# Two Strassen pairs in place of four plain blocks in a decoder layer's output projection

## The chip, the cores and the metric

One core of one Trainium2 chip runs the whole kernel. The metric is the device time of one execution in microseconds (us); the time of the kernel before is the median of three runs. The engines are written as in the profile: PE (TensorE's matmuls), PEld (its weight loads), DVE (VectorE), ACT (ScalarE), POOL (GpSimd) and SP (which issues the weight transfers). Each runs its own list of instructions strictly in order and waits on the others through semaphores.

## The reference, cut to what matters

A decoder layer for 256 tokens, width 2048: a SwiGLU feed-forward, a mixer of attention and a gated recurrence, a second SwiGLU feed-forward, a gated embedding. The part that changes is the end of the mixer and the way into the second feed-forward:

```python
merged = sigmoid(gate_a) * (out_a @ w_up_a) + sigmoid(gate_b) * (out_b @ w_up_b)   # 256 x 2048
x = x + merged @ w_out                                                            # 2048 x 2048
h = rmsnorm(x, ffn2_norm)                                                         # mean over 2048
x = x + 0.5 * (silu(h @ w_gate) * (h @ w_up)) @ w_down                            # 5632 wide
```

## The kernel before, in words

Tokens are two tiles of 128 (t = 0, 1); the 2048 columns of x are four blocks of 512 (nb = 0 to 3), each of them two SBUF tiles x[0][nb] and x[1][nb]. All weights are f32 and arrive on SP's queue as tiles `raw` of 128x1024: 256 rows of the weight by 512 columns. To keep f32 accuracy each operand is split in two fp32r parts: ACT casts a weight to `whi` (line 127), DVE subtracts to get `wlo` (line 128), and the product is act_hi·whi + act_lo·whi + act_hi·wlo. Rings of buffers limit how far this runs ahead: 8 raw tiles, 5 whi and 5 wlo. So the cast of weight i+5 has to wait until PE has read whi of a weight that is done with. `Weights.next` prepares up to 4 weights ahead (AHEAD), and one call of it also runs the tasks that `W.later(n, ...)` has put n weights into the future.

There are two ways to multiply.

- `block_a` makes one block of 512 columns in two PSUM banks of the ring `acc` (4 banks), with 12 matmuls of 128x512 for each weight tile.
- `strassen_group` makes two blocks at once (gate and up of a feed-forward, or two neighbouring blocks). The contraction is cut in four quarters by PATTERN "PSPS". A P quarter is plain: 4 weight tiles, 12 matmuls each. An S quarter is Winograd's form of Strassen's method on 2 x 2 x 2 sub-blocks: seven products ("roles") instead of eight, each with 6 matmuls, so 42 instead of 48; four of the weights in it are sums, which DVE forms in place (line 111), and the seven split weights again need whi and wlo. Its activations (`A.roles`) include four sums too, in hi and lo (tiles `as`). The group has eight accumulators: P1, P2, Q3, Q6 in the ring `acc` and Q7, Q5, P4, PE in the ring `misc` (4 banks too, shared with all transposes). At its end ACT copies P1 and DVE combines the banks (lines 422 and 432) into the result.

The norm before the second feed-forward is hidden as follows. `scaled_stage` takes the sum of squares of each finished x block on ACT (`square_sum`, line 275). After three of the four blocks it forms a provisional scale s3 from the three (lines 546 to 549), and `scaled_parts` scales x by it (`xs`, line 371), transposes it on PE (`tx`, line 363), multiplies by the gain and splits into hi and lo (`ap`), for quarters 0, 1 and 2; quarter 3 follows after the fourth block. The exact factor, the full rms over s3, is applied later to the outputs of the feed-forward.

The order of the instructions on each engine comes from the scheduler of the framework, which lists them by priority and by its own estimates and gives out the buffers of a ring in that order; the weight preparation has a raised priority. The order is fixed before the kernel runs.

Of the kernel before, what the change touches and what calls it, by code (L numbers as in the profile page):

```python
# [10 lines left out]
F32 = mybir.dt.float32  # L11
# [4 lines left out]
ALU = mybir.AluOpType  # L16
AX = mybir.AxisListType
# [133 lines left out]
GATES = ((0, 1), (), (2,), (3,))  # L151


def weight_order():
# [49 lines left out]
    for nb in range(4):  # L204
        block("w_out", nb)
# [11 lines left out]
def decoder_layer(ctx: ExitStack, tc: tile.TileContext, io, out):  # L217
# [148 lines left out]
    def scaled_parts(A, q, s, gain, kind):  # L366
# [22 lines left out]
        if kind == "P":  # L389
            return  # L390
        a11, a21, a12, a22 = (quarter[:, k, :, t] for k in range(2) for t in range(2))
        a5, a6, a7, a3 = (full[1][:, i] for i in range(4))
# [3 lines left out]
        nc.scalar.copy(hi, full[1])  # L396
        nc.vector.tensor_tensor(lo, full[1], hi.bitcast(F32), op=ALU.subtract)
        raw = lambda k, t: lambda c: tuple(A.plain[q][k][:, c, h, t * P:(t + 1) * P] for h in range(2))
        mix = lambda i: lambda c: (hi[:, i, c], lo[:, i, c])
        A.roles[q] = (raw(0, 0), raw(1, 0), mix(3), mix(1), mix(2), mix(0), raw(1, 1))  # L400
# [133 lines left out]
    def scaled_stage(stage, gain):  # L534
# [390 lines left out]
    mT = {}  # L925
    sga, sgb = {}, {}
    A2, on_block, left2 = scaled_stage("f2", gains["ffn2"])
    for nb in range(4):
# [174 lines left out]
```

## Time and profile before

| | |
|---|---|
| median of 3 runs | 2187.78 us (2187.15 to 2188.99) |
| the profiled execution | 2186.81 us, of which the span 2184.9 us |
| busy in the span: PE, PEld | 2164.2 us (99%), 1779.4 us (81%) |
| busy in the span: DVE, ACT | 1756.6 us (80%), 1208.0 us (55%) |
| output projection (w_out), PE | 1274.8 to 1366.6 us |
| the second feed-forward's first group on PE | 1366.6 to 1408.5 us |

A busy PE counts overlapped matmuls: one lasts about 0.39 us in the records, and the next one starts about 0.23 us after it. What a stage costs is therefore read from the distance of starts. Rows of the timeline give start, duration, engine, line, operation, names out<-in, shapes, how many were merged, and in brackets the engine's idle time before and what ended it.

### The profile page before, as it was taken

What the parts mean: (1) busy time and instruction counts of PE and PEld (TensorE: products, weight loads), DVE (VectorE), ACT (ScalarE), POOL (GpSimd) and SP (SyncE); (2) the same over time, 40 slices, a digit from 0 to 9 for tenths busy, and PEclk for the clock granted to TensorE, in tenths of its full rate; (3) what the DMA queues carried; (4) which work ended last, traced back from release to release, by engine and by line L of the source; (5) the groups of instructions that cost most, each with busy time, mean ns of one, the idle gap of its engine ahead of it and who ended that gap; (6) DMA issues with size and microseconds to landing.
All of it is one profiled execution on the core that took longest, in us unless ns stands there. A gap on an engine that the chain in (4) does not pass through costs nothing.

```text
span 2184.9 us, 28075 instructions
## 1 busy us (share of the span) xinstructions
PE 2164.2 (99%) x10352; PEld 1779.4 (81%) x10352; DVE 1756.6 (80%) x2066; ACT 1208.0 (55%) x1547; POOL 14.0 (1%) x28
## 2 busy tenths in 40 slices
PE   8999999999999999999999999999999999999998
PEld 7888888888888888887888888878888888888877
DVE  7997979789796998787664556998896979889586
ACT  8554645445456666556444445665554545555664
POOL 0000000000000000000000000000000000000000
PEclk9999999999999999999999999999999999999999
DMA  9464655646466447444565665447555464656552
GB/s 339 164 231 156 233 165 218 220 166 231 157 245 194 161 178 249 146 129 147 155 192 187 190 191 180 167 170 249 185 215 183 176 210 172 246 182 219 175 196 101
DMA packets 117928, 418.96 MB, mean 192 GB/s; under 512 B 13728, under 2 KB 13984, under 8 KB 117792
## 3 DMA queue, kind: packets, MB, share of 16 engines
q1 hardware_dynamic: 116928, 415.83, 56.1%
q8 instruction: 81, 1.33, 0.2%
q10 hardware_dynamic: 864, 1.35, 0.2%
q14 instruction: 55, 0.45, 0.1%
HBM read 415.03 MB, written 2.10 MB: 191 GB/s over the span
## 4 chain that ended last, share of the span: by engine, by line
PE 95%; DVE 2%; DMA 1%; issue 1%; ACT 1%; SPq 0%; POOL 0%; ACTq 0%; POOLq 0%; DVEq 0%
PE ps L419 45%; PE pa L310 14%; PE pa L311 14%; PE pa L316 14%; PE pb L331 3%; PE pb L333 1%; DVE wlo L128 1%; PE tp L353 1%; PE lv L847 1%; PE tx L363 1%; ACT whi L127 0%; DMA raw<-in_ffn_up 0%; PE sc L765 0%; DMA raw<-in_ffn_gate 0%; DMA x<-in_x 0%
## 5 line engine op out<-in xcount | busy, mean ns | idle before, releaser
L127 ACT CAST whi<-raw 128x1024 fp32r<-128x1024 f32 (+1 forms) x931 | 951.1, 1052 | 806.2 <-PE pa L311 385.8
L128 DVE TENSOR_TENSOR wlo<-raw,whi 128x1024 fp32r<-128x1024 f32 (+1 forms) x931 | 1101.5, 1219 | 326.5 <-ACT whi L127 316.7
L419 PE MATMUL ps<-whi,ap 128*128 128x512 f32 x2200 | 573.9, 391 | 2.5 <-DVE ff L422 2.1
L419 PEld LDWEIGHTS ps<-whi,ap 128*128 128x128 f32 x2200 | 410.2, 188 | 91.3 <-DVE ff L422 6.8
L419 PE MATMUL ps<-wlo,ap 128*128 128x512 f32 x1100 | 314.4, 390 | 0.1
L310 PE MATMUL pa<-whi,act 128*128 128x512 f32 x704 | 274.4, 392 | 0.0
L311 PE MATMUL pa<-whi,act 128*128 128x512 f32 x704 | 273.7, 391 | 0.0
L111 DVE TENSOR_TENSOR raw<-raw,raw 128x1024 f32<-128x1024 f32 x200 | 244.6, 1223 | 5.1
L419 PEld LDWEIGHTS ps<-wlo,ap 128*128 128x128 f32 x1100 | 206.3, 188 | 43.3 <-DVE wlo L128 0.5
L419 PE MATMUL ps<-whi,as 128*128 128x512 f32 x800 | 213.8, 391 | 0.9 <-ACT whi L127 0.9
L316 PE MATMUL pa<-wlo,act 128*128 128x512 f32 x704 | 193.9, 391 | 0.0
L419 PEld LDWEIGHTS ps<-whi,as 128*128 128x128 f32 x800 | 149.1, 188 | 35.4 <-ACT whi L127 3.7
L310 PEld LDWEIGHTS pa<-whi,act 128*128 128x128 f32 x704 | 132.0, 188 | 27.5 <-ACT act L355 0.6
L311 PEld LDWEIGHTS pa<-whi,act 128*128 128x128 f32 x704 | 132.1, 188 | 27.1 <-DVE act L356 0.4
L316 PEld LDWEIGHTS pa<-wlo,act 128*128 128x128 f32 x704 | 131.9, 188 | 26.9
L310 PE MATMUL pa<-whi,ap 128*128 128x512 f32 (+1 forms) x384 | 144.7, 381 | 0.0
L311 PE MATMUL pa<-whi,ap 128*128 128x512 f32 (+1 forms) x384 | 141.5, 373 | 0.0
L422 DVE TENSOR_TENSOR ff<-ps,ff 128x512 f32<-128x512 f32 x200 | 128.1, 682 | 0.8
L419 PE MATMUL ps<-wlo,as 128*128 128x512 f32 x400 | 123.5, 390 | 0.0
L316 PE MATMUL pa<-wlo,ap 128*128 128x512 f32 (+1 forms) x384 | 97.6, 372 | 0.0
L419 PEld LDWEIGHTS ps<-wlo,as 128*128 128x128 f32 x400 | 74.9, 188 | 16.0 <-DVE wlo L128 0.6
L310 PEld LDWEIGHTS pa<-whi,ap 128*128 128x128 f32 x384 | 72.4, 189 | 14.1 <-issue 1.1
(250 smaller groups left out, 1740.8 us busy)
## 6 DMA issues: line engine op xcount, KB each, us to landing
raw<-in_ffn_up SPq DMA_DIRECT2D x176, 512.0 KB, 5.2
raw<-in_ffn_down SPq DMA_DIRECT2D x176, 512.0 KB, 5.4
raw<-in_ffn_gate SPq DMA_DIRECT2D x175, 512.0 KB, 4.5
raw<-in_w_ga SPq DMA_DIRECT2D x32, 512.0 KB, 3.5
raw<-in_w_gb SPq DMA_DIRECT2D x32, 512.0 KB, 3.5
raw<-in_w_out SPq DMA_DIRECT2D x32, 512.0 KB, 3.5
raw<-in_ple_gate SPq DMA_DIRECT2D x32, 512.0 KB, 4.6
raw<-in_w_i SPq DMA_DIRECT2D x16, 512.0 KB, 4.2
```

Of the source, the lines that this page charges most:

```text
L111: add = lambda out, a, b: nc.vector.tensor_tensor(out, a, b, op=ALU.add)
L127: nc.scalar.copy(hi[:, c], src[:, c])
L128: nc.vector.tensor_tensor(lo[:, c], src[:, c], hi[:, c].bitcast(F32), op=ALU.subtract)
L310: nc.tensor.matmul(ps[t], ks[:, 0, tok], hi[:, c], start=(j == 0 and c == 0), stop=False)
L311: nc.tensor.matmul(ps[t], ks[:, 1, tok], hi[:, c], start=False, stop=False)
L316: nc.tensor.matmul(ps[t], ks[:, 0, tok], lo[:, c], start=False, stop=(last and c == 1))
L331: nc.tensor.matmul(ps, hi[:, c], mov(c), start=(first and c == 0), stop=False)
L333: nc.tensor.matmul(ps[:, 0:S], lo[:, c], mov(c)[:, 0], start=False, stop=False)
L353: nc.tensor.transpose(pt[:, c, t * P:(t + 1) * P], srcs[t][:, i * P:(i + 1) * P], ident)
L363: nc.tensor.transpose(pt[:, c, t * P:(t + 1) * P], srcs[t][:, i * P:(i + 1) * P], ident)
L419: nc.tensor.matmul(bank(i), stat, mov, start=done[i] == 1, stop=done[i] == todo(i))
L422: nc.vector.tensor_tensor(out, banks[b], other, op=op)
```

## The change

The output projection runs as two `strassen_group` calls: blocks 0 and 1, then blocks 2 and 3. For that `merged` in transposed and split form (tiles mT) is kept as `Operands`, and `role_parts` makes the four activation sums of the S quarters from it (quarter 1 during the up-projections, quarter 3 during the first group). Four weights become seven in each S quarter, so 44 prepared weights take the place of 32. `scaled_stage` gets a parameter: for the second feed-forward the provisional scale now covers the first two blocks (the first group), quarters 0 and 1 are made during the second group, and quarters 2 and 3 after it, during the feed-forward's first group. The two other uses of `scaled_stage` are unchanged.

```diff
+LATE = (3, 3, 3, 2)
...
-    for nb in range(4):
-        block("w_out", nb)
+    for nb in (0, 2):
+        pair(("w_out", nb), ("w_out", nb + 1))
...
+    def role_parts(A, q):
+        full, sums = (atile([P, 4, 2, P], F32, name="af") for _ in range(2))
+        quarter = full.rearrange("p (k c) t n -> p k c t n", k=2)
+        for kp in range(2):
+            v = A.plain[q][kp].bitcast(F32)
+            nc.vector.tensor_tensor(quarter[:, kp].rearrange("p c t n -> p c (t n)"), v[:, :, 0], v[:, :, 1], op=ALU.add)
+        A.roles[q] = sum_parts(A, q, quarter, sums)
...
-            if nb == 2:
-                nc.vector.tensor_reduce(v3, ss[:, :, 0:3], axis=AX.X, op=ALU.add)
-                nc.vector.tensor_scalar(v3, v3, 1.0 / 1536, EPS, op0=ALU.mult, op1=ALU.add)
+            if nb == first - 1:
+                nc.vector.tensor_reduce(v3, ss[:, :, 0:first], axis=AX.X, op=ALU.add)
+                nc.vector.tensor_scalar(v3, v3, 1.0 / (512 * first), EPS, op0=ALU.mult, op1=ALU.add)
...
-                for q in range(3):
+                for q in range(first):
                     W.later(1 + 2 * q, lambda q=q: scaled_parts(A, q, s3, gain, PATTERN[q]))
...
-                W.later(2, lambda: scaled_parts(A, 3, s3, gain, PATTERN[3]))
+                for q in range(first, 4):
+                    W.later(q - 1, lambda q=q: scaled_parts(A, q, s3, gain, PATTERN[q]))
...
-    A2, on_block, left2 = scaled_stage("f2", gains["ffn2"])
+    A2, on_block, left2 = scaled_stage("f2", gains["ffn2"], 2)
...
+        mO.plain[nb] = [atile(name="mT") for _ in range(2)]
         for kp in range(2):
-            mT[2 * nb + kp] = m = atile(name="mT")
-            W.later(3 + kp, lambda m=m, e=e, kp=kp: transpose_split(m, e, kp))
-    for nb in range(4):
-        ps = block_a("w_out", nb, lambda k: mT[k // 2][:, k % 2])
-        for t in range(2):
-            nc.vector.tensor_tensor(x[t][nb], ps[t], x[t][nb], op=ALU.add)
-        on_block(nb)
+            W.later(LATE[nb] + kp, lambda nb=nb, e=e, kp=kp: transpose_split(mO.plain[nb][kp], e, kp))
+        if PATTERN[nb] == "S":
+            W.later(LATE[nb] + 2, lambda nb=nb: role_parts(mO, nb))
+    for nb in (0, 2):
+        def merged(d, t, second, nb=nb):
+            nc.vector.tensor_tensor(x[t][nb + second], d[:, t], x[t][nb + second], op=ALU.add)
+
+        strassen_group(("w_out", nb), ("w_out", nb + 1), mO, PATTERN, merged)
+        on_block(nb)
+        on_block(nb + 1)
```

SP's list of transfers keeps its order to the last row. On PE, DVE and ACT the lists differ only between the end of the up-projections and the first quarters of the second feed-forward. Lines below the new LATE are numbered one higher in the change, those of `strassen_group` 13 higher (L422 is L435, L419 is L432), and L964 is the addition to x. Weights are numbered through: in the change 526 to 547 are the first pair of w_out, 548 to 569 the second, and 570 to 591 the first group of the second feed-forward.

**First place: PE, where the transposes of the scaled x stand.** Before, in w_out's last block (weights 550 to 557, banks pa), after the norm over three blocks:

```order
L316 MATMUL pa_584_11248<-wlo551_11187,mT_527_9661 128x512
L316 MATMUL pa_585_11249<-wlo551_11187,mT_527_9661 128x512
L363 MATMUL tx_590_11262<-ident_64,xs_586_11256 128x128
L363 MATMUL tx_591_11271<-ident_64,xs_586_11256 128x128
L310 MATMUL pa_584_11248<-whi552_11204,mT_536_9832 128x512
L311 MATMUL pa_584_11248<-whi552_11204,mT_536_9832 128x512
```

Two weights of the block, 24 matmuls, stand between the third block's end and the first transpose. In the change, at the start of the second pair (ps_604 and ps_606 are P2 and Q3 in the ring acc, ps_605 and ps_607 are P4 and PE in the ring misc, which the tx tiles share):

```order
L432 MATMUL ps_604_11189<-whi548_11088,mT_526_9660 128x512 x4
L432 MATMUL ps_604_11189<-wlo548_11089,mT_526_9660 128x512 x2
L432 MATMUL ps_604_11189<-whi550_11114,mT_527_9661 128x512 x4
L432 MATMUL ps_604_11189<-wlo550_11115,mT_527_9661 128x512 x2
L432 MATMUL ps_606_11207<-whi549_11101,mT_526_9660 128x512 x4
L432 MATMUL ps_606_11207<-wlo549_11102,mT_526_9660 128x512 x2
L432 MATMUL ps_606_11207<-whi551_11132,mT_527_9661 128x512 x4
L432 MATMUL ps_606_11207<-wlo551_11133,mT_527_9661 128x512 x2
L432 MATMUL ps_618_11296<-whi552_11161,mT_536_9832 128x512 x4
```

```order
L432 MATMUL ps_606_11207<-wlo554_11222,as_544_9936 128x512 x2
L432 MATMUL ps_619_11334<-whi555_11274,as_544_9936 128x512
L364 MATMUL tx_602_11171<-ident_64,xs_598_11165 128x128
L364 MATMUL tx_603_11180<-ident_64,xs_598_11165 128x128
L364 MATMUL tx_602_11171<-ident_64,xs_599_11166 128x128
L364 MATMUL tx_602_11171<-ident_64,xs_598_11165 128x128
```

Each of the first four weights is used for one of its two token tiles only, then 552, 553, 554 and one matmul of 555 follow, then the eight transposes, and only behind them the other halves of 548 to 551 (in ps_605 and ps_607). Until those are done, 548 to 551 hold four of the five whi buffers. The start of the second feed-forward's first group has the same form: 42 matmuls (570 to 573 for one token tile, 574 to 576), then two transposes of x's block 2.

**Second place: DVE around the provisional norm.** Before, after w_out's third block:

```order
L949 TENSOR_TENSOR x12_79<-pa_581_11093,x12_79 128x512
L128 TENSOR_TENSOR wlo555_11295<-raw555_11202,whi555_11294 128x1024
L546 TENSOR_REDUCE v3f2_8541<-ssf2_8539 128x2
L547 TENSOR_SCALAR v3f2_8541<-v3f2_8541 128x2
L549 TENSOR_TENSOR v3f2_8541<-v3f2_8541,s3f2_8540 128x2
L128 TENSOR_TENSOR wlo556_11313<-raw556_11220,whi556_11312 128x1024
```

In the change, after the first pair (L435 forms the last combination, L111 the sums of weights of the next S quarter):

```order
L128 TENSOR_TENSOR wlo553_11204<-raw553_11112,whi553_11203 128x1024
L964 TENSOR_TENSOR x11_78<-ff_575_10787,x11_78 128x512
L435 TENSOR_TENSOR ff_574_10786<-ps_578_10798,ff_574_10786 128x512
L128 TENSOR_TENSOR wlo554_11222<-raw554_11130,whi554_11221 128x1024
L964 TENSOR_TENSOR x10_77<-ff_574_10786,x10_77 128x512
L111 TENSOR_TENSOR raw554_11130<-raw555_11159,raw554_11130 128x1024
L111 TENSOR_TENSOR raw555_11159<-raw552_11099,raw555_11159 128x1024
L559 TENSOR_REDUCE v3f2_8541<-ssf2_8539 128x2
L111 TENSOR_TENSOR raw552_11099<-raw552_11099,raw554_11130 128x1024
L560 TENSOR_SCALAR v3f2_8541<-v3f2_8541 128x2
L111 TENSOR_TENSOR raw553_11112<-raw553_11112,raw552_11099 128x1024
L128 TENSOR_TENSOR wlo555_11275<-raw552_11099,whi555_11274 128x1024
```

The last addition to x (x10) now stands behind wlo554, and the reduction stands ahead of the sum that weight 555 is made of.

**Third place: ACT there.** Before:

```order
L127 CAST whi555_11294<-raw555_11202 128x1024
L275 ACTIVATE junk_583_11242,ssf2_8539<-x12_79 128x512
L371 ACTIVATE xs_586_11256<-x00_73,s3f2_8540 128x512
L127 CAST whi556_11312<-raw556_11220 128x1024
L371 ACTIVATE xs_587_11257<-x10_77,s3f2_8540 128x512
```

In the change:

```order
L127 CAST whi553_11203<-raw553_11112 128x1024
L127 CAST whi554_11221<-raw554_11130 128x1024
L276 ACTIVATE junk_592_11146,ssf2_8539<-x10_77 128x512
L276 ACTIVATE junk_593_11148,ssf2_8539<-x01_74 128x512
L276 ACTIVATE junk_594_11150,ssf2_8539<-x11_78 128x512
L127 CAST whi555_11274<-raw552_11099 128x1024
L372 ACTIVATE xs_598_11165<-x00_73,s3f2_8540 128x512
L372 ACTIVATE xs_599_11166<-x10_77,s3f2_8540 128x512
```

Three sums of squares, the cast of 555 and two scalings of x now stand in a row behind the cast of 554.

More of the change, by code (lines that the diff above doesn't have):

```diff
@@ L390, in scaled_parts, with sum_parts @@
             return
+        A.roles[q] = sum_parts(A, q, quarter, full[1])
+    def role_parts(A, q):
[5 more added lines that the diff above has]
+        A.roles[q] = sum_parts(A, q, quarter, sums)
+    def sum_parts(A, q, quarter, sums):
         a11, a21, a12, a22 = (quarter[:, k, :, t] for k in range(2) for t in range(2))
-        a5, a6, a7, a3 = (full[1][:, i] for i in range(4))
+        a5, a6, a7, a3 = (sums[:, i] for i in range(4))
         for o, u, v in ((a5, a21, a22), (a6, a11, a5), (a7, a21, a11), (a3, a12, a6)):
@@ L395, in scaled_parts @@
         hi, lo = (atile([P, 4, 2, P], name="as") for _ in range(2))
-        nc.scalar.copy(hi, full[1])
-        nc.vector.tensor_tensor(lo, full[1], hi.bitcast(F32), op=ALU.subtract)
+        nc.scalar.copy(hi, sums)
+        nc.vector.tensor_tensor(lo, sums, hi.bitcast(F32), op=ALU.subtract)
         raw = lambda k, t: lambda c: tuple(A.plain[q][k][:, c, h, t * P:(t + 1) * P] for h in range(2))
         mix = lambda i: lambda c: (hi[:, i, c], lo[:, i, c])
-        A.roles[q] = (raw(0, 0), raw(1, 0), mix(3), mix(1), mix(2), mix(0), raw(1, 1))
+        return (raw(0, 0), raw(1, 0), mix(3), mix(1), mix(2), mix(0), raw(1, 1))
     def strassen_group(first, second, A, pattern, post):
@@ L532, in ffn, with scaled_stage @@
                     on_block(nb)
-    def scaled_stage(stage, gain):
+    def scaled_stage(stage, gain, first=3):
         ss = const.tile([P, 2, 4], F32, name=f"ss{stage}")
```

2 lines of the change are left out of this document (1 added, 1 removed).

## The prediction

> **What bounds the kernel now.** I read the page's engine shares, its chain of waits and its costliest groups first, then the busy times of the two stages that change, then the timeline at three places.
>
> ```profile
> PE 2164.2 (99%) x10352; PEld 1779.4 (81%) x10352; DVE 1756.6 (80%) x2066; ACT 1208.0 (55%) x1547; POOL 14.0 (1%) x28
> PE 95%; DVE 2%; DMA 1%; issue 1%; ACT 1%; SPq 0%; POOL 0%; ACTq 0%; POOLq 0%; DVEq 0%
> 1274.60:1366.60 92.00, 91.38 (x418) 75.26 (x417) 53.61 (x62) 49.02 (x68) 0.69 (x1) 1.00 0.59 183
> 1366.60:1408.00 41.40, 41.40 (x187) 34.17 (x187) 37.48 (x40) 27.25 (x36) 0.70 (x1) 1.00 0.42 146
> 1408.00:1450.00 42.00, 41.07 (x183) 33.02 (x182) 41.21 (x43) 24.88 (x28) 0.00 (x0) 1.00 0.53 195
> ```
>
> The last three rows are windows: stretch, its length, busy PE, PEld, DVE, ACT, POOL, then the granted clock. PE sets the end. In w_out (first window) it never stops, and DVE works 53.6 of 92 us; in the groups of the second feed-forward (the other two) DVE works 91 and 98% of the time. So the change moves a stage from the first kind to the second, and both engines must be costed. What a matmul costs:
>
> ```profile
> 1299.38 1.07 PE L316 MATMUL pa<-wlo,mT 128*128 128x512 f32 x4
> 1302.10 1.07 PE L316 MATMUL pa<-wlo,mT 128*128 128x512 f32 x4
> ```
>
> From one weight's wlo part to the next one's is 2.72 us for 12 matmuls: 0.227 us each.
>
> **What it saves.** 32 weights of 12 matmuls are 384; the two groups have 2 x (4 x 12 + 7 x 6) = 180 each, 360. 24 matmuls at 0.227 are **-5.4 us**. Transposes stay 40 in both (8 of merged, 32 of x).
>
> **What it adds to DVE and ACT.** 12 more weights to split, 16 sums of weights, 16 combinations of banks and two sets of activation sums.
>
> ```profile
> L128 DVE TENSOR_TENSOR wlo<-raw,whi 128x1024 fp32r<-128x1024 f32 x65 | 75.0, 1218 | 3.8 <-ACT whi L127 3.6
> L111 DVE TENSOR_TENSOR raw<-raw,raw 128x1024 f32<-128x1024 f32 x24 | 29.3, 1221 | 0.4
> 1405.88 5.76 DVE L128 TENSOR_TENSOR wlo<-raw,whi 128x1024 fp32r<-128x1024 f32 x5
> 1411.56 4.39 DVE L422 TENSOR_TENSOR ff<-ps,ff 128x512 f32<-128x512 f32 x7
> ```
>
> Five splits in 5.76 us start 1.14 us apart; seven combinations in 4.39 us start 0.62 apart; a sum of weights takes 1.22. A steady group of the change, from its first combination to the next group's, has on DVE 22 splits (25.0), 8 sums (9.8), 12 combinations and additions to x (7.4) and the norm and splits of two quarters of x (about 6): 48.2 us, where PE needs 180 x 0.227 = 40.8 plus 16 transposes. So DVE has no slack to repay a late start. For the first group role_parts comes on top (about 4 us) with fewer combinations; the 3.9 us that DVE idled in the second window cover that, and I cost it at 0 (up to 2 if not). ACT gets 12 casts, two copies of a bank and two casts of sums, 16 us, where it worked 49 of 92: nothing away from the joints. The raw transfers stay 32, in the same order.
>
> **What is late: the two joints.** Between two groups the kernel before already waits once:
>
> ```profile
> 1406.89 0.57 ACT L432 COPY ff<-ps 128x512 f32<-128x512 f32 x1
> 1407.37 2.01 ACT L127 CAST whi<-raw 128x1024 fp32r<-128x1024 f32 x2
> 1408.48 1.07 PE L419 MATMUL ps<-whi,ap 128*128 128x512 f32 x4
> 1412.30 1.20 PE L419 MATMUL ps<-whi,ap 128*128 128x512 f32 x4 [0.93 <-DVE ff L422]
> ```
>
> The next group starts at 1408.48. DVE starts the combinations 3.1 us later (1411.56, above), behind the splits of five more weights. PE does 12 matmuls (2.7 us) and needs a bank that the first combination frees: it goes on 3.8 us after the start, 1.1 us late. In the change this joint carries the norm too. Its parts:
>
> ```profile
> 1285.54 0.39 PE L311 MATMUL pa<-whi,mT 128*128 128x512 f32 x1
> 1285.97 1.05 ACT L127 CAST whi<-raw 128x1024 fp32r<-128x1024 f32 x1 [1.27 <-PE pa L311]
> 1287.05 1.23 DVE L128 TENSOR_TENSOR wlo<-raw,whi 128x1024 fp32r<-128x1024 f32 x1 [1.39 <-ACT whi L127]
> 1369.62 0.63 ACT L275 ACTIVATE junk<-x 128x512 f32<-128x512 f32 x1
> 1370.24 1.32 ACT L371 ACTIVATE xs<-x,s3f 128x512 f32<-128x512 f32 x2
> 1370.89 0.15 DVE L280 TENSOR_REDUCE rstdf<-ssf 128x2 f32<-128x8 f32 x1
> 1371.33 0.70 POOL L282 TENSOR_TENSOR rstdf<-rstdf,nhalf 128x2 f32<-128x2 f32 x1 [24.82 <-DVE rstdf L281]
> ```
>
> A cast starts 0.43 us after the start of the last matmul that read its buffer, the split 1.08 after the cast; squares and scalings (junk, xs) take 0.62 each; the reduction 0.15, the power 0.70.
>
> First joint, T = 0 where weight 548 starts, by the lists shown with the change. 548 and 550 run to 2.7, then PE waits to 3.8; 549 and 551 end at 6.5. 548 to 551 keep four whi buffers, so weights now pass one at a time through the fifth: 552's last read of whi starts at 7.2; cast of 553 at 7.65, split at 8.7 (DVE has just done nine combinations and additions, 3.1 + 9 x 0.62 = 8.7); 553's last read at 9.4; cast of 554 at 9.9; DVE does x11 and the last combination to 11.1, the split of 554 to 12.2, x10 to 12.9. ACT squares x10, x01, x11 to 14.9. The reduction goes at 15.0, the sum that 555 needs to 16.3, its cast to 17.4 (the power runs beside it), the two scalings to 18.7, the eight transposes to about 19.4. By then PE has done 43 matmuls and 8 transposes. For a transpose:
>
> ```profile
> L363 PE MATMUL tx<-ident,xs 128*128 128x128 f32 x24 | 3.6, 280 | 0.6 <-ACT xs L371 0.6
> ```
>
> 3.6 us for 24 is 0.15 each, so the work is 9.75 + 1.2 = 10.95 and 8.5 us are lost. Behind it the last four transposes need a misc bank whose DVE reads come behind a split, about 0.5 more: **+9.0 us**.
>
> Second joint, same clock: x12 at 12.9; three squares, the last started at 14.2; first scaling 14.8 to 15.5, second to 16.1 (the factor is known, so no power). The two first transposes start at 15.5 where PE has 42 matmuls (9.5) behind it; with the six others it is at 16.9 for 44 matmuls and 8 transposes, 11.2: 5.7 lost. Then quarter 3's second scaling stands behind two casts and two splits on ACT (0.4), and the cast and split of 580 are late by 0.55 and 0.4: **+7.1 us**. Both sums contain the usual 1.1.
>
> Smaller terms. Before, PE waited 0.6 us for xs (the row above): -0.6. In block 2's up-projections the gate's copy out of its bank (`nat`) now comes four casts later, since it waits for a buffer of the ring of 23 that role_parts fills; so the next product takes the bank that DVE frees behind the last matmul:
>
> ```profile
> 1263.91 0.69 DVE L938 TENSOR_TENSOR mg<-pa,nat 128x512 f32<-128x512 f32 x1 [1.09 <-PE pa L316]
> ```
>
> That read takes 0.69: +0.7, between 0 and 1.
>
> The clock. At the first joint PE idles from 12.9 to 17.5, 4.6 us.
>
> ```profile
> 5.84 0.79 PE L310 MATMUL pa<-whi,hTf 128*128 128x512 f32 x1 [5.84 <-ACT whi L127]
> 6.86 0.63 PE L310 MATMUL pa<-whi,hTf 128*128 128x512 f32 x1
> 7.29 0.63 PE L311 MATMUL pa<-whi,hTf 128*128 128x512 f32 x1
> 9.01 0.40 PE L311 MATMUL pa<-whi,hTf 128*128 128x512 f32 x1
> 2175.25 0.40 PE L316 MATMUL pa<-wlo,ap 128*128 128x256 f32 x2
> 2178.00:2180.00 2.00, 0.00 (x0) 0.00 (x0) 1.30 (x5) 0.83 (x2) 0.55 (x1) 0.95 0.00 0
> 2180.00:2182.00 2.00, 0.00 (x0) 0.00 (x0) 0.05 (x1) 0.50 (x1) 0.00 (x0) 0.50 0.78 294
> ```
>
> After the last matmul (ended 2175.65) the granted clock halves at 2179.8 (0.95 over two us means 1.8 us full), 4.15 us later; matmuls at the very start are 0.43 apart, not 0.227, from 5.84 to about 9.0 us. So the first joint may restart at half rate, 0 to +1.5 us, of which I take **+1.0**; the second idles 2.6 us and should keep its clock, 0. The Trainium skill, "TensorE: Matmul & The Clock Gate", section "What's actually happening", says that the clock falls after at least one idle window of about 3.4 us and that the window runs free. By this the first joint surely pays its 1.5, and the sum would be 0.5 higher; the row here gives a longer delay, so the measured one counts.
>
> **The sum**: -5.4 + 9.0 + 7.1 - 0.6 + 0.7 + 1.0 = **+11.8 us**. Against the profiled execution, 2186.8 (span 2184.9 and 1.9 around it), this is 2198.6; the median of the runs is 1.0 higher, so 2199.6. Bounds of the joints: 1.1 each (the joint before, below), and half-rate restarts in both (2.0 more) with 2 us of late DVE behind each (6 more in all, above). SP's transfers wait for raw buffers that are freed later, not earlier, and land ahead of their use as now.
>
> **The rivals.** *A, forecast: the norm's chain holds PE at both joints*, 2199.6. For it: PE works in order, and the transposes stand ahead of half of four weights. *B, not slower: the scaled x is there when PE gets to the transposes.* The place is the first transpose, the point that decides 9.75 us after the group's end (9.5 at the second); the price is then 1.1 at each joint: -5.4 - 0.6 + 2.2 + 0.7 = -3.1, 2184.7. The kernel before speaks for it, where 24 matmuls nearly covered such a chain; against it, there the chain was without two casts, a split and three additions that wait for a late combination. Its best case, with no wait at all, is 2182.5. *C: DVE's throughput is the bound, not the chain.* Then the second pair and the feed-forward's first group take 48.2 each, the first 41.9 + 0.7; together 139.0, where 91.8 + 41.9 = 133.7 stood: +5.3, 2193.1. For it, the 98% of the last window; against it, DVE itself waits in the chain. *D: the joints are longer*, both restart at half rate and DVE comes later still: +6, about 2206. *E: the compiled work is not what it says*, ruled out by the lists.
>
> **How the numbers follow.** A 0.68, B 0.08, C 0.13, D 0.11. The measurement tells about 0.2% (4.4 us) from no change. Faster needs B's best end: 0.03. Same holds the rest of B and the low end of C: 0.08. Slower: 0.89. The range takes in A and its bounds, most of C and of D: 2191 to 2206; A's own is 2195 to 2203.
>
> **What would show it.** In the profile after: w_out and the first feed-forward group together about 146 us (133.7 before); two PE idle stretches before `tx` of 4 to 5 and 2 to 3 us, released by xs, each with two shorter ones before it, released by whi; the row of tx (L364) with some 7 us of idle, 0.6 before; a granted clock below 1 in the stretch of the first joint; w_out's first pair at about 42 us. If PE passes the transposes without an idle stretch, A is wrong; if DVE is busy all through the joints, it is C.

## The result, and the profile after

The change makes the kernel slower: 2202.78 us in the median of four runs (2201.43 to 2204.20), where the kernel before took 2187.47 beside it. The ratio is 1.0069, with an interval of 1.0057 to 1.0081. That is +15.3 us against a forecast of +11.8; 2202.8 lies in the range (2191 to 2206) and in forecast A's own range (2195 to 2203). Why it is so late is another matter: in the change PE is held as A said, but when e1 below takes that hold away, another wait takes its place and most of the loss stays.

The profiled execution of the change took 2204.06 us with a span of 2202.1. Its first row of engine shares:

```profile
PE 2168.7 (98%) x10328; PEld 1777.7 (81%) x10328; DVE 1805.3 (82%) x2124; ACT 1221.7 (55%) x1563; POOL 16.0 (1%) x28
```

The 24 matmuls less are there (10352 before), and DVE has 48.7 us more to do. The three groups as windows (stretch, length, busy PE, PEld, DVE, ACT, POOL, granted clock): the first pair of w_out, the second pair, and the feed-forward's first group, each from the first matmul of one group to that of the next.

```profile
1276.40:1318.31 41.91, 41.91 (x189) 34.46 (x188) 40.18 (x42) 23.84 (x27) 0.00 (x0) 1.00 0.43 148
1318.31:1373.11 54.80, 47.52 (x198) 36.91 (x196) 48.07 (x57) 32.77 (x47) 1.66 (x1) 0.94 0.46 157
1373.11:1425.77 52.66, 46.75 (x197) 35.98 (x196) 48.01 (x57) 32.68 (x47) 1.66 (x1) 0.97 0.45 159
```

Together 149.4 us, where the prediction had about 146 and the kernel before 133.7. The first pair runs at PE's pace, and the loss sits in the two others. A group needs 180 x 0.227 + 16 x 0.15 = 43.3 us of PE, so they lose 11.5 and 9.4. DVE works 48.07 and 48.01 us in them; the prediction counted 48.2.

The waits of PE in the second pair and then in the next group, from the timeline (start, us, what, and in brackets the idle time before it with its releaser):

```profile
1321.92 1.20 PE L432 MATMUL ps<-whi,mT 128*128 128x512 f32 x4 [0.72 <-DVE ff L435]
1327.02 1.20 PE L432 MATMUL ps<-whi,mT 128*128 128x512 f32 x4 [0.73 <-ACT whi L127]
1336.07 0.80 PE L432 MATMUL ps<-whi,as 128*128 128x512 f32 x1 [4.68 <-ACT whi L127]
1337.49 2.15 PE L364 MATMUL tx<-ident,xs 128*128 128x128 f32 x8 [0.62 <-ACT xs L372]
...
1376.91 1.20 PE L432 MATMUL ps<-whi,ap 128*128 128x512 f32 x4 [0.92 <-DVE ff L435]
1382.04 1.20 PE L432 MATMUL ps<-whi,ap 128*128 128x512 f32 x4 [0.73 <-ACT whi L127]
1388.87 0.44 PE L364 MATMUL tx<-ident,xs 128*128 128x128 f32 x2 [2.46 <-ACT xs L372]
1397.27 0.60 PE L432 MATMUL ps<-wlo,ap 128*128 128x512 f32 x1 [0.81 <-DVE wlo L128]
```

It is the forecast picture: a bank first, then weights one at a time through the fifth whi buffer, then the long wait around the transposes. The first tx stands 19.2 us behind the group's start at the first joint and 15.8 at the second; the prediction had both scalings ready at 18.7, and the second joint's first two transposes at 15.5.

Two things are new. The clock (last but two of a window's columns) halves behind both joints, and the power takes 1.66 us where it took 0.70 before:

```profile
1337.50:1341.50 4.00, 4.00 (x13) 3.27 (x14) 1.45 (x3) 3.20 (x7) 0.00 (x0) 0.50 0.45 131
1397.00:1399.00 2.00, 1.73 (x7) 1.50 (x8) 1.11 (x4) 1.70 (x3) 0.00 (x0) 0.63 0.92 352
1399.00:1401.00 2.00, 2.00 (x6) 1.60 (x5) 0.59 (x1) 0.78 (x2) 0.00 (x0) 0.51 0.67 236
```
```profile
1335.02 1.66 POOL L561 TENSOR_TENSOR s3f<-v3f,nhalf 128x2 f32<-128x2 f32 x1 [245.27 <-DVE v3f L560]
1390.04 1.66 POOL L283 TENSOR_TENSOR rstdf<-rstdf,nhalf 128x2 f32<-128x2 f32 x1 [53.36 <-DVE rstdf L282]
```

The wait in block 2's up-projection came as well:

```profile
1199.16 0.47 PE L311 MATMUL pa<-whi,ob 128*128 128x512 f32 x1 [0.65 <-DVE mg L952]
```

### The profile page after: what moved, and what is told of

It is laid out like the page before. It is cut to its first block, busy times and chain, and to the rows that moved or that the text cites. A ratio compares the mean times of both kernels' runs of the same rounds, so it can differ in the third digit from the quotient of the medians.

```text
span 2202.1 us, 28128 instructions
## 1 busy us (share of the span) xinstructions
PE 2168.7 (98%) x10328; PEld 1777.7 (81%) x10328; DVE 1805.3 (82%) x2124; ACT 1221.7 (55%) x1563; POOL 16.0 (1%) x28
## 5 line engine op out<-in xcount | busy, mean ns | idle before, releaser
L127 ACT CAST whi<-raw 128x1024 fp32r<-128x1024 f32 (+1 forms) x943 | 962.0, 1051 | 796.7 <-PE pa L312 347.5
L128 DVE TENSOR_TENSOR wlo<-raw,whi 128x1024 fp32r<-128x1024 f32 (+1 forms) x943 | 1114.3, 1220 | 296.7 <-ACT whi L127 287.6
L432 PE MATMUL ps<-whi,ap 128*128 128x512 f32 x2200 | 575.6, 392 | 4.2 <-DVE ff L435 2.8
L432 PEld LDWEIGHTS ps<-whi,ap 128*128 128x128 f32 x2200 | 410.5, 188 | 93.9 <-DVE ff L435 7.7
L432 PE MATMUL ps<-wlo,ap 128*128 128x512 f32 x1100 | 315.6, 390 | 1.2 <-DVE wlo L128 1.1
L111 DVE TENSOR_TENSOR raw<-raw,raw 128x1024 f32<-128x1024 f32 x216 | 264.3, 1223 | 5.5
L432 PEld LDWEIGHTS ps<-wlo,ap 128*128 128x128 f32 x1100 | 206.5, 188 | 45.3 <-DVE wlo L128 2.5
L432 PE MATMUL ps<-whi,as 128*128 128x512 f32 x864 | 231.7, 391 | 6.4 <-ACT whi L127 6.4
L432 PEld LDWEIGHTS ps<-whi,as 128*128 128x128 f32 x864 | 161.0, 188 | 44.4 <-ACT whi L127 11.5
L435 DVE TENSOR_TENSOR ff<-ps,ff 128x512 f32<-128x512 f32 x216 | 138.2, 682 | 0.8
L432 PE MATMUL ps<-wlo,as 128*128 128x512 f32 x432 | 133.5, 390 | 0.1
L432 PEld LDWEIGHTS ps<-wlo,as 128*128 128x128 f32 x432 | 80.8, 188 | 18.2 <-DVE wlo L128 1.6
```

The source lines that it names most:

```text
L111: add = lambda out, a, b: nc.vector.tensor_tensor(out, a, b, op=ALU.add)
L127: nc.scalar.copy(hi[:, c], src[:, c])
L128: nc.vector.tensor_tensor(lo[:, c], src[:, c], hi[:, c].bitcast(F32), op=ALU.subtract)
L432: nc.tensor.matmul(bank(i), stat, mov, start=done[i] == 1, stop=done[i] == todo(i))
L435: nc.vector.tensor_tensor(out, banks[b], other, op=op)
```

## The experiments

**The theories.** A: PE's own list holds it, because the transposes of x stand ahead of half of four weights and wait for the norm's chain. C: DVE has 48 us of work for each of two groups, and the groups can't be shorter. The first run takes the transposes out of PE's way, the second the last links of the norm's chain; both leave DVE its work. The medians of the kernel before differ by up to 1.3 us from round to round (2187.29 to 2188.56), so a difference of 1 to 2 us between runs of different rounds says little.

**e1: the transposes later.** In the change, for the second feed-forward alone:

```diff
-                    W.later(1 + 2 * q, lambda q=q: scaled_parts(...))   # q = 0, 1: 1, 3
+                    W.later(due[q], lambda q=q: scaled_parts(...))      # 3, 5
-                    W.later(q - 1, lambda q=q: scaled_parts(...))       # q = 2, 3: 1, 2
+                    W.later(due[q], lambda q=q: scaled_parts(...))      # 3, 5
```

> The scaled quarters of the second feed-forward are asked for two or three weights later, nothing else is changed. In PE's list the second token halves of weights 548 to 551 and of 570 to 573 then stand ahead of the transposes of x, so whi buffers come free one after the other, and some 130 matmuls (30 us) at the first joint and 66 (15 us) at the second stand between the group's start and the first tx. If PE was held by the place of the transposes in its list (forecast A), both joints shrink to the usual 1.1 us: before's 2187.5 - 5.4 - 0.6 + 2.2 + 0.8 = 2184.5, the granted clock stays at 1.00, and w_out with the first feed-forward group takes 41.9 + 43.2 + 43.2 = 128 to 132 us (149.4 in the change). If DVE's throughput is what holds it (C), the second pair and the first group still take 48 us each: about 2193. If the waits come from DVE's and ACT's late start alone, whatever PE's order, the time stays at 2201 to 2204.

Measured: 2201.33 us (ratio 1.0063, 1.0050 to 1.0075). A's number is missed by 17 us. The first joint does become short (its waits on PE are 1.1, 1.3, 0.9, 0.8 and 0.7 us from one matmul's start to the next), and no tx is waited for longer than 0.32 us. But then PE stops at the second joint. PE's row there, and DVE's rows of the same time:

```profile
1372.81 2.07 PE L432 MATMUL ps<-whi,ap 128*128 128x512 f32 x4 [7.37 <-ACT ff L445]
```
```profile
1359.89 10.30 DVE L128 TENSOR_TENSOR wlo<-raw,whi 128x1024 fp32r<-128x1024 f32 x9
...
1373.45 1.28 DVE L435 TENSOR_TENSOR ff<-ps,ff 128x512 f32<-128x512 f32 x2
```

The first weight of the next group waits for a bank of this one. ACT's copy out of it (L445) and DVE's combinations (L435) stand behind nine splits and the last sums of x's parts, which have themselves become later. From its start to that of the next one, the second pair takes 55.2 us and the group behind it 48.2; of these 103.3 us DVE works 93.6. The four matmuls in the row take 2.07 us where such a row takes 1.2, since the clock is halved again:

```profile
1372.50:1378.50 6.00, 5.69 (x13) 4.18 (x14) 5.82 (x9) 1.34 (x4) 0.00 (x0) 0.50 0.26 105
```

**e2: the scaled x without x and its norm.** Here the requests stay as in the change, and in the second feed-forward the scaled x is made of a constant:

```diff
-            nc.scalar.activation(xs[t], x[t][q], AF.Copy, scale=s[:, t:t + 1])
+            nc.scalar.activation(xs[t].rearrange("p (a n) -> p a n", a=4), ones.unsqueeze(1).to_broadcast([P, 4, P]),
+                                 AF.Copy, scale=nhalf[:, t:t + 1])
```

> Left out: the second feed-forward's transposed input is made of a constant instead of the scaled x (same scalings, transposes, splits and sums, so the output is wrong); the norm itself is still computed. The scaling then waits for no addition, no square and no power, while the transposes stay where the change has them, ahead of the second token halves. Forecast A: the two long waits before tx go (5.1 and 2.9 us), with the waits on whi behind them, about 1.1 us per joint stays: 2184 to 2187. C (DVE's throughput): 48 us for each of the two groups, about 2193. If the fifth whi buffer alone holds PE, not the chain of the norm, the tx passes at once and little else changes: about 2195.

Measured: 2199.33 us (1.0057, 1.0042 to 1.0072), 12 us above A's range. But the edit takes away less than was expected of it: the scalings need nothing of x any more, and yet they stand behind the three squares in ACT's list, and these wait for the late additions to x. ACT's rows at the first joint, here and then in the change:

```profile
1331.46 0.63 ACT L276 ACTIVATE junk<-x 128x512 f32<-128x512 f32 x1 [1.89 <-DVE x L967]
...
1333.32 1.93 ACT L373 ACTIVATE xs<-ones,nhalf 128x512 f32<-128x512 f32 x3
```
```profile
1336.71 2.56 ACT L372 ACTIVATE xs<-x,s3f 128x512 f32<-128x512 f32 x4 [0.69 <-POOL s3f L561]
```

So only its last links leave the chain (the reduction, the power, and the cast of 555 that stood ahead of the scalings), and only at the first joint; at the second one the factor was known in the change too. Two of its waits, and the second pair and the next group as windows:

```profile
1334.08 0.44 PE L364 MATMUL tx<-ident,xs 128*128 128x128 f32 x2 [2.46 <-ACT xs L373]
1385.91 1.22 PE L435 MATMUL ps<-whi,as 128*128 128x512 f32 x2 [5.64 <-ACT whi L127]
```
```profile
1318.52:1367.85 49.33, 44.61 (x198) 34.67 (x197) 46.88 (x57) 31.91 (x46) 1.65 (x1) 1.00 0.46 161
1367.85:1421.52 53.67, 46.69 (x198) 36.30 (x196) 48.80 (x57) 32.91 (x48) 0.70 (x1) 0.94 0.47 169
```

The first tx stands 15.6 us behind the group's start instead of 19.2, the clock stays full there, and the second pair takes 49.3 us (54.8 in the change). The group behind it takes 53.7, one more than in the change. At the second joint the cast of weight 577 waits for sums of weights on DVE, which stand there among combinations and additions to x: 5.64 us, longer than any wait of the change there (and two matmuls of 577 now stand ahead of the first tx). What the first joint gives back is partly lost at the second. Since PE still waits for xs behind the additions to x, e2 doesn't price A's chain as a whole; it says that those last links are worth some 3 us in all, the full clock behind the first joint included.

**e3 and e4: each part alone.** The kernel before with only the smaller norm (first = 2 and the two quarters behind block 3), and the change with the norm over three blocks:

```diff
-    A2, on_block, left2 = scaled_stage("f2", gains["ffn2"])       # e3, w_out in plain blocks
+    A2, on_block, left2 = scaled_stage("f2", gains["ffn2"], 2)
```
```diff
-    A2, on_block, left2 = scaled_stage("f2", gains["ffn2"], 2)    # e4, w_out in two groups
+    A2, on_block, left2 = scaled_stage("f2", gains["ffn2"])
```

> The kernel before with only the second part of the change: the provisional norm covers two blocks and two quarters are asked for behind block 3; w_out keeps its four plain blocks. There the additions to x follow a block's last matmul at once, so the chain is short: A expects 2187 to 2189 (0 to +1.5; one more quarter is transposed in the feed-forward's first group). If the smaller norm is what costs (a late second quarter of two), about 7 us more: 2194.

> The change with only its first part: w_out in two Strassen groups, the provisional norm over three blocks as before, so nothing of it is asked for at the first joint. A expects the first joint to shrink to the usual 1.1 us (11.6 less than measured in the change) and the whole chain, power and all four quarters, to fall on the second one, where PE has four matmuls ahead of the first transpose: 20 to 25 us lost instead of 10.6, so 2201 to 2206 in all, the same as the change. If the smaller norm brings the loss into w_out and nothing takes its place, 2191.

Measured: 2187.26 us (0.9998, 0.9989 to 1.0007) and 2206.38 us (1.0087, 1.0073 to 1.0100). The norm alone costs nothing: x is waited for as long as in the kernel before (0.62 us, the row below). Without it the pairs are dearer still. That wait of e3, and of e4 the longest wait and the second pair, from its start to the end of its matmuls:

```profile
1326.57 0.44 PE L363 MATMUL tx<-ident,xs 128*128 128x128 f32 x2 [0.62 <-ACT xs L371]
```
```profile
1375.23 2.15 PE L364 MATMUL tx<-ident,xs 128*128 128x128 f32 x8 [12.38 <-ACT xs L372]
1319.59:1362.69 43.10, 41.50 (x181) 33.39 (x179) 42.38 (x43) 24.67 (x32) 0.00 (x0) 1.00 0.56 204
```

So the loss comes with the pairs, and the smaller norm takes some 3.6 us off it by dividing the chain between two joints. e4 also speaks for A's account of what PE waits for: with nothing of the norm at the first joint, the second pair runs at almost PE's pace (DVE works 42.4 of its 43.1 us), and the whole chain, 12.38 us of waiting for xs, comes at the second joint. The time is 0.4 above the 2201 to 2206 that A expected.

**e5 and e6: less work on DVE.** Sixteen of the 44 splits of the two groups are left out, once in e1 and once in the change:

```diff
+FREE = (*range(560, 568), *range(582, 590))
-            hi, lo = self.tile("whi", i, 5), self.tile("wlo", i, 5)
+            hi = self.tile("whi", i, 5)
+            lo = hi if i in FREE else self.tile("wlo", i, 5)
...
+                if i not in FREE:               # around the subtraction that makes lo
```

> The kernel with the later transposes, and 16 of the 44 DVE splits left out in the two groups (weights 560 to 567 and 582 to 589: the matmuls read whi where they would read wlo, as many matmuls as before, so the output is a little wrong). That takes 16 x 1.14 = 18 us from DVE, whose work of 48 us a group falls to 39, below PE's 42. If DVE's work is what the two groups wait for (C), the 7.8 us stop at the second joint and the one behind it go, and the time falls from 2201.3 to 2184 to 2187. If the stops come from the order of ACT's and DVE's lists at the joint, not from the amount, half of it stays: 2193 to 2197. If PE's own list still holds it, nothing changes: 2200 to 2202.

> The change as it is, with the same 16 DVE splits left out (late weights of the two groups, behind the joints' chains). Forecast A: PE is held only at the joints, by the chain of the norm with the transposes ahead of the second token halves, and runs without a stop in between, so what DVE saves there is idle time: 2200 to 2203. C (DVE's amount of work alone): 2186 to 2190. If both bounds lie close to each other, the first joint keeps its 12 us and the second one, which DVE reaches with less left to do, gives some back: 2194 to 2199.

Measured: 2196.50 us (1.0035, 1.0021 to 1.0048) and 2199.37 us (1.0050, 1.0035 to 1.0065): 4.8 less than e1, 3.4 less than the change. e5 lies where the order of ACT's and DVE's lists was expected to put it. e6 lies between A (from 2200) and the case in which both bounds are close (to 2199). C alone gives neither. In e6 the second pair as a window, and the waits before the transposes of the two joints:

```profile
1319.07:1373.68 54.61, 47.37 (x198) 36.78 (x196) 41.05 (x51) 33.37 (x48) 1.65 (x1) 0.94 0.47 167
```
```profile
1336.82 0.79 PE L435 MATMUL ps<-whi,as 128*128 128x512 f32 x1 [4.68 <-ACT whi L129]
...
1386.40 0.44 PE L367 MATMUL tx<-ident,xs 128*128 128x128 f32 x2 [0.47 <-ACT xs L375]
```

DVE works 41.1 us instead of 48.1, and the pair takes 54.6 us, 0.2 less than in the change: what DVE does behind the joint doesn't set the pair's end, and what PE loses it loses at the joint, as A says. Only the second one, which DVE reaches with less left over, gets shorter (0.47 us idle before tx instead of 2.46). In e5 the chain is away and DVE has less to do, and the second joint still waits, because the combinations keep their place behind seven splits:

```profile
1370.05 1.20 PE L435 MATMUL ps<-whi,ap 128*128 128x512 f32 x4 [3.06 <-ACT ff L448]
```
```profile
1362.92 8.04 DVE L131 TENSOR_TENSOR wlo<-raw,whi 128x1024 fp32r<-128x1024 f32 x7 [1.26 <-ACT whi L129]
...
1372.01 1.28 DVE L438 TENSOR_TENSOR ff<-ps,ff 128x512 f32<-128x512 f32 x2
```

**e9 and e10: place, and place with amount.** The evictions of w_out's two groups get a raised priority, in e1 and in e5:

```diff
-                steps.pop(0)[1]()
+                with tc.high_priority(offset=PRIO + 1000 if early else 0):   # early: w_out's groups
+                    steps.pop(0)[1]()
```

> The kernel with the later transposes, and in w_out's two groups the copies, combinations of banks and additions to x get the raised priority of the transposed parts, above that of the weights. Nothing else is changed. If the 7.8 us stop at the second joint of the kernel with later transposes comes only from the places of DVE's and ACT's rows (eight splits ahead of the combinations), it shrinks to 1 to 3 us and the half clock behind it goes: 2190 to 2194. If DVE's amount of work (48 us a group where PE needs 42) sets the end, another wait takes its place: 2197 to 2201.

> Both at once: later transposes, raised priority of the combinations, and the same 16 DVE splits left out (whi is read in place of wlo, so the output is wrong). If place in the list and amount of work on DVE together are the whole loss, the two groups run at PE's pace: 2184 to 2188 (2187.5 - 5.4 - 0.6 + 2.2 + 0.8 = 2184.5). If something else holds PE at the joints (the ring of 23 activation buffers, ACT), it stays at 2193 to 2196.

Measured: 2198.19 us (1.0048, 1.0031 to 1.0065) and 2186.87 us (0.9996, 0.9987 to 1.0006). With DVE's whole work the priority gives 3.1 us. At the first joint PE no longer waits for a bank. At the second one the priority hardly moves the combinations: nine splits still stand ahead of them, as in e1. PE waits there again, 3.24 us and then 1.27 and 1.01 (7.37 in e1), and the clock is halved behind it. PE's and DVE's rows of e9 there, and its second pair to the end of its matmuls:

```profile
1370.45 1.20 PE L432 MATMUL ps<-whi,ap 128*128 128x512 f32 x4 [3.24 <-ACT ff L446]
```
```profile
1361.62 10.30 DVE L128 TENSOR_TENSOR wlo<-raw,whi 128x1024 fp32r<-128x1024 f32 x9
...
1372.98 1.28 DVE L435 TENSOR_TENSOR ff<-ps,ff 128x512 f32<-128x512 f32 x2
```
```profile
1319.21:1367.04 47.83, 44.56 (x197) 34.40 (x195) 44.29 (x52) 29.27 (x44) 1.66 (x1) 1.00 0.49 171
```

With 16 splits less the loss is gone. The two groups of e10, and DVE's first rows at its second joint:

```profile
1318.02:1365.86 47.84, 44.57 (x198) 34.75 (x197) 40.00 (x50) 32.34 (x49) 1.66 (x1) 1.00 0.54 189
1365.86:1409.99 44.13, 43.37 (x198) 34.98 (x196) 38.84 (x48) 32.76 (x46) 0.70 (x1) 1.00 0.57 199
```
```profile
1359.54 0.69 DVE L438 TENSOR_TENSOR ff<-ps,ff 128x512 f32<-128x512 f32 x1 [1.34 <-ACT ff L449]
...
1360.88 2.35 DVE L131 TENSOR_TENSOR wlo<-raw,whi 128x1024 fp32r<-128x1024 f32 x2
```

That is 92.0 us instead of the change's 107.5, at full clock. But not only the amount is different from e9. The scheduler, which knows of the missing splits, now puts the first combination of the second joint ahead of all the splits that it stood behind, and most of the others behind three. The second pair's own matmuls take the same time in both (47.8 us), although 8 of the missing splits belong to that pair; what differs comes behind them.

The four runs with later transposes make a square: 2201.3 with neither edit (e1), 2198.2 with the priority (e9), 2196.5 with fewer splits (e5), 2186.9 with both (e10). Alone they give 3.1 and 4.8 us, together 14.5. So once the transposes are out of the way, the rest of the loss goes with the place of the combinations and DVE's work together, and only in part with either alone. How much of it is the amount and how much the place was not taken apart, because the missing splits change the place as well.

**e7: the clock.** Filler matmuls in the idle time ahead of the transposes of both joints:

```diff
+        if fill:                                    # 5 for q = 0, 3 for q = 2
+            pf = misc([P, 512], uid("fill"))
+            for i in range(fill):
+                nc.tensor.matmul(pf, ident, x[1][q], start=i == 0, stop=i == fill - 1)
```

> The change with filler on PE: 5 and 3 matmuls (fp32, 128x512, on the x block that DVE adds last, into a spare bank) ahead of the first transposes of the two joints; about 0.9 us each, they fit into the idle time of 5.1 and 2.9 us. The granted clock should then stay at 1.00 behind both joints. If half rate is a price of its own, the 14 matmuls and 12 transposes that ran at 0.43 and 0.21 us instead of 0.23 and 0.11 give back 3 to 4 us: 2198 to 2200. If DVE catches up meanwhile and sets the end anyway, the time stays at 2202 to 2203. If the filler delays the transposes, 2204 and more.

Measured: 2199.98 us (1.0054, 1.0040 to 1.0068), 2.8 less than the change. The filler, the transposes behind it, and the stretches behind the two joints:

```profile
1332.20 4.56 PE L376 MATMUL fill<-x,ident 128*128 128x512 f32 x10
1338.42 0.44 PE L364 MATMUL tx<-ident,xs 128*128 128x128 f32 x2 [0.44 <-ACT xs L372]
```
```profile
1337.50:1341.50 4.00, 3.56 (x21) 2.69 (x20) 1.26 (x3) 3.86 (x7) 0.11 (x1) 1.00 0.42 131
1396.00:1400.00 4.00, 4.00 (x19) 3.31 (x18) 3.15 (x4) 4.00 (x8) 0.00 (x0) 1.00 0.69 200
```

The transposes come as late as before: the first wait of the pair starts them 15.6 us behind it in both kernels (1338.42 - 1322.86 here, 1337.49 - 1321.92 above). But the clock stays full, so half rate is a price of its own. Between the two profiled executions it is 4.6 us of span (2202.1 to 2197.5), between the medians 2.8. The four runs with filler lie within 0.2 us (2199.91 to 2200.08), those of the change at 2201.4 to 2201.5 and 2204.1 to 2204.2. That one of the two half-rate stretches comes and goes between executions would fit; only one of those executions has a trace, so it isn't shown.

**e8: half of the change.** Blocks 0 and 1 as a pair, blocks 2 and 3 plain, the norm over three blocks:

```diff
-    for nb in (0, 2):
-        pair(("w_out", nb), ("w_out", nb + 1))
+    pair(("w_out", 0), ("w_out", 1))
+    for nb in (2, 3):
+        block("w_out", nb)
```

> Half of the change: w_out's blocks 0 and 1 as a Strassen group, blocks 2 and 3 plain, the norm over three blocks as before. 12 matmuls less (-2.7); the one new joint stands before plain blocks, which leave DVE idle (53.6 of 92 us before), and the second joint is the one of the kernel before. Under A and under C alike: 2187.3 - 2.7 + 1.1 (bank at the joint) + 0.8 (block 2's up-projection) = 2186.5, 2185.5 to 2188. If a Strassen group is by itself dearer than its matmuls say, 2190 and more.

Measured: 2186.03 us, where the kernel before took 2188.23 beside it (0.9991, 0.9982 to 1.0000). From the start of w_out to the second group of the feed-forward, with half a microsecond to spare at both ends:

```profile
1275.00:1409.00 134.00, 133.34 (x605) 109.29 (x604) 116.33 (x134) 83.98 (x113) 1.39 (x2) 1.00 0.51 178
```

PE idles 0.7 us in all. The pair's combinations fall beside plain blocks, where DVE has room, and of the 1.1 us for a bank at the joint about 0.3 is paid. It is the best version found; at 0.1% it stays below what a measurement tells from no change.

**e11: why the power takes 1.66 us.** In e1, one power of two columns of wlo for each weight:

```diff
+    W.probe = lambda lo: nc.gpsimd.tensor_tensor(probe, ones[:, 0:2], lo[:, 0:2].bitcast(F32), op=ALU.pow)
```

> The kernel with the later transposes, with one more power (128x2, of a column of wlo, into a scratch tile) on the otherwise idle POOL for each weight from the up-projections on; the output is as before. The power of the norm took 0.70 us before and 1.66 at both joints of the change. If DVE's fp32 operations that read and write SBUF (splits, sums of weights) hold POOL up, the powers that run beside such an operation take 1.2 to 1.7 us and those beside an idle DVE or beside reads of PSUM 0.70. If the 1.66 has another cause, all take about 0.70.

Measured in one execution, 2219.7 us: the norm's own power stands behind the probes in POOL's queue, and PE waits longer at both joints, so the time says nothing. The durations do. A probe with DVE idle beside it, three beside a row of splits, and those splits:

```profile
1561.57 0.70 POOL L943 TENSOR_TENSOR probe<-ones,wlo 128x2 f32<-128x2 f32 x1 [2.16 <-DVE wlo L129]
```
```profile
1500.88 5.76 DVE L129 TENSOR_TENSOR wlo<-raw,whi 128x1024 fp32r<-128x1024 f32 x5
1502.25 3.81 POOL L943 TENSOR_TENSOR probe<-ones,wlo 128x2 f32<-128x2 f32 x3 [6.91 <-DVE wlo L129]
```

Of the 512 probes the 110 that ran with nothing on DVE took 0.69 to 0.70 us. The 235 mostly beside a split took 1.24 in the mean, and the 16 beside an addition that reads one operand from PSUM (x<-pa,x) 0.70. The power at the joints is late because it runs beside splits and sums of weights.

**e12: can POOL take work from DVE?** In e9, the additions to x and the subtractions of the activation sums:

```diff
-            nc.vector.tensor_tensor(x[t][nb + second], d[:, t], x[t][nb + second], op=ALU.add)
+            nc.gpsimd.tensor_tensor(x[t][nb + second], d[:, t], x[t][nb + second], op=ALU.add)
-            nc.vector.tensor_tensor(o, u, v, op=ALU.subtract)
+            (nc.gpsimd if A.pool else nc.vector).tensor_tensor(o, u, v, op=ALU.subtract)
```

> The kernel with later transposes and raised combinations, and DVE's eight additions to x and the subtractions of the four sets of activation sums of w_out and the second feed-forward moved to the idle POOL (same computation). That takes about 3.8 us a group from DVE (4 x 0.60 and 4 x 0.35). If DVE's amount of work sets the end, the time falls from 2198.2 by most of 7.6: 2190 to 2194. If POOL's rows, which DVE's work beside them slows (0.70 to 1.66 us for a power), come too late for the norm and the transposes, that is eaten up: 2196 to 2201.

Measured: 2207.26 us (1.0087, 1.0074 to 1.0101), 9 slower than e9 and beyond both expectations. POOL's group of additions, and five splits on DVE beside three of them:

```profile
L968 POOL TENSOR_TENSOR x<-ff,x 128x512 f32<-128x512 f32 x8 | 15.9, 2010 | 42.9 <-DVE ff L436 42.9
```
```profile
1325.28 8.08 DVE L129 TENSOR_TENSOR wlo<-raw,whi 128x1024 fp32r<-128x1024 f32 x5
```

An addition takes POOL 2.0 us where DVE needs 0.68, and five splits take 8.08 us instead of 5.76. DVE loses on its own rows what it was to gain: its splits last 1.37 us in the mean from w_out to the first feed-forward group, 1.22 in e9. The additions stand in the norm's chain besides, and PE waits 4.38 us for xs at the first joint, 1.19 in e9.

## Why the prediction was right, and where it was not

- **The saving (-5.4).** Right: 24 matmuls less in the page's count.
- **The first joint (+9.0) and the second (+7.1).** Right in size. They measured 11.5 and 9.4, together 20.9; e7 puts the clock's part at 3.0 and 1.9 (its two groups take 51.8 and 50.8 us instead of 54.8 and 52.7), so 16.0 are left, where the terms were 16.1. Within the first, the power ran 0.96 longer than the 0.70 taken.
- **The clock (+1.0 and 0).** Mis-sized: about 4.9 in the profiled execution, 2.8 by the medians. The step that failed is "the second idles 2.6 us and should keep its clock". Its longest idle time was 2.46 us (the row at 1388.87), and it lost it, 8.7 us after that had ended. Nor was "0 to +1.5" wide enough for the first. The rule of the Trainium skill weighed there ("TensorE: Matmul & The Clock Gate", section "What's actually happening", a fall after at least one idle window of some 3.4 us) agrees with the first joint, where the stop is 4.68 us; the second joint differs from it, if it is read as one stretch without a matmul, and the measurement counts.
- **The smaller terms.** Block 2's wait (+0.7) measured 0.8 (a matmul 1.04 us behind the one before it instead of 0.23). role_parts at 0 held: the first pair took 41.91, forecast 41.9.
- **"PE works in order, and the transposes stand ahead of half of four weights"** as the reason. Right for the change as it stands: with 7 us less on DVE the first of the two groups is only 0.2 us shorter (e6), and with nothing of the norm at the first joint that joint is short and the second one long (e4). It is not the price: with the transposes out of the way (e1) only 1.5 us come back, which is hardly clear of the rounds' differences, and not the 15 that separate A from B.
- **Rival C, 2193.1.** Its DVE work was counted right (48.2; 48.07 measured), but it was priced as if DVE could work without a pause, 96.4 us for the two groups. In e1, where A's hold is away, they took 103.3: 93.6 of work and 9.7 in which DVE waited, though PE waited for DVE elsewhere. That is 6.9 on 2193.1, so 2200.0, and 2201.33 was measured. Priced so, after the fact, C would have stood level with A: they are two bounds of nearly the same length. The sentence "DVE has no slack to repay a late start" pointed there, but no rival put the two bounds together.
- **Rival B, 2184.7.** Its condition, x in time for the transposes, was met in e1 but for 0.32 us, and was not enough. e10, which has in addition less work on DVE and its combinations in front, came to 2186.87.
- **Rivals D and E.** Both joints did get a stretch at half rate, as D had it, though at the second one it came 8.7 us behind the restart; its other half, a DVE later than in A, was not needed. E stayed ruled out.
- **"What would show it".** The two idle stretches, their releasers, the shorter ones before them and the clock were as written. The row of tx was not: of its 7 us only 3.2 stand there, since most of the first stop is booked to the one matmul of weight 555 that stands ahead of the transposes. That row, for the two groups:

```profile
L364 PE MATMUL tx<-ident,xs 128*128 128x128 f32 x32 | 6.5, 334 | 3.2 <-ACT xs L372 3.1
```

What stays open: what of the 11.3 us between e9 and e10 is DVE's amount of work and what the place of the combinations, and whether a schedule exists that keeps both pairs with DVE's whole work and reaches the kernel before. e9 and e12 were two attempts, and neither did.

## What to carry to other kernels

A wait at the end of a chain shows what came last, not what it costs: before a stall is priced, add up the work of the engine the chain runs through over the whole stage, with its pauses (in the change 48 us on DVE and 4.7 to 6.7 us in which it waits, for 43 on PE), because that bound can stand right behind, as it did here. An edit that trades matmuls for additions needs room on the engine for the additions, so try it first beside stages that leave it idle: one pair before plain blocks ran without a stall, two pairs in a row cost 15 us. And where PE will stall, count a stretch at half clock behind it; here even waits of at most 2.46 us had one.

## What the runs showed of the hardware that was not expected

- **The clock halved without a long stop.** At the second joint of the change PE's longest idle time was 2.46 us (before tx at 1388.87), and the granted clock fell to half at about 1397.5, 8.7 us later, for 3.4 us. Filler in the idle time kept it at 1.00 at both joints.
- **POOL and DVE hold each other up.** A power of 128x2 takes 0.70 us alone and 1.66 beside DVE operations with two operands in SBUF, while DVE's splits kept their 1.22. An addition of 128x512 on POOL does slow DVE: a split beside it took up to 2.31 us. The Trainium skill, "SBUF — State Buffer", section "Who interferes with whom", says that a DVE instruction with two SBUF inputs contends with a GpSimd instruction that reads SBUF, one with at most one such input doesn't; the traces agree on both (1.66 beside splits and sums of weights at the joints, 0.70 beside x<-pa,x in e11).
